# A two-layer diffusion backbone on one core: the modulation loads reordered, and the work at the end of layer 0 and in the second attention placed anew

## The chip, the cores and the metric

The kernel runs on one core of one Trainium2 chip. The metric is the device time of one execution in microseconds (us). A core has a matrix engine (TensorE, PE in the profile), a vector engine (VectorE, DVE), a scalar engine (ScalarE, ACT), a general engine (GpSimd, POOL), and a queue that issues the transfers (SyncE, SP). Each engine runs its own instructions in order; semaphores let one wait for another.

## What is computed

1024 latent tokens and 256 context tokens of width 1024 pass through two layers, in float32. Layer 0 is a global attention A with rotary positions and a banded attention B, side by side; layer 1 is a convolution module C and a neighbourhood attention D with a table of position biases. Only latent tokens leave layer 1, through a last normalisation.

```
for i in range(DEPTH):                       # DEPTH = 2
    sh_l, sc_l, g_l = modulation(c, mod_w[i], mod_b[i])      # silu(cond) @ w + b, in thirds
    sh_c, sc_c, g_c = modulation(c_ctx, mod_w[i], mod_b[i])
    h_lat = rms_norm(x_lat, norm_g[i]) * (1.0 + sc_l) + sh_l
    h_ctx = rms_norm(x_ctx, norm_g[i]) * (1.0 + sc_c) + sh_c
    if i % 2 == 0:
        y_lat, y_ctx = even_mixer(h_lat, h_ctx, ...)   # A and B: projections, softmax(q k) v, gate, @ w_out
    else:
        y_lat, y_ctx = odd_mixer(h_lat, h_ctx, ...)    # C and D: conv + layer norm, attention + bias, gate, @ w_out
    x_lat = x_lat + g_l * y_lat
    x_ctx = x_ctx + g_c * y_ctx              # layer 0 only
return rms_norm(x_lat, final_g)
```

## The kernel before

Every matrix product of the projections is made of three (`mm3`, lines 363 to 365): each factor is split into a rounded high part and the remainder (`split`, lines 334 and 337: hh and hl, wh and wl, ph and pl), and high by high, low by high and high by low are summed. The high part is a copy on ACT; the low part is a subtraction on POOL or DVE.

Tokens go in three chunks, c = 0 (256 context tokens), 1 and 2 (512 latent tokens each). In the opening, x and the modulation weights (mw) arrive by transfers that SP issues, in the order of the letters of `PLAN`: `a`, `b`, `c` and `v` are steps of four slices of the modulation (a capital finishes one), digits load a chunk of x, `n` asks for the squares and sums of a chunk, `w` loads projection weights, `r` makes the broadcast reciprocal root, `H` and `h` make the normalised chunk, `q` projects chunk 0. A chunk's way: squares on ACT (lines 758 to 771), sums acc on DVE or POOL (762, 772), a product with ones on PE (trs), rbv on DVE (293), nr, the power -1/2, on POOL (274), its broadcast bc on PE (299), x·g·bc on DVE (351), and then per block of 128 channels either hh on ACT and hl on DVE (`HV` has a `v`, line 355) or both by `split` on ACT and POOL (`g`). modT is the transposed modulation, made by PE (trm) from mrow, which ACT copies.

Attention (`attn_gen`) runs over groups of tiles. A tile is a score st on PE (lines 531 and 535, from QH, QL and the key table KAt), an exponential pf on ACT, its split ph and pl, and, three tiles later, three products with the values into ov (472 to 474). Every `vshare`-th low part is on DVE, the others on POOL. At the end of a group DVE transposes the sums out of ov (r, line 482), multiplies by the gate (y, or yu in layer 1) and frees the bank. Before a group its maxima are found (`maxes`: products mx on PE, maxima mp on DVE, their negative nmt, transposed by PE, and QL on DVE, line 430; Q goes through memory to QH); this preparation starts `LEAD` tiles after the start of the group two before.

Other work is woven in: `weave(main, n, fill, m)` takes n steps of the attention and spreads m steps of the fill over them: the projections of the next head unit (`NFILL`), the output projection of layer 0 (`O1`), layer 1's projections and output (`WV`, with `LAG`, the number of score tiles that the fill may run ahead). At build time a scheduler fixes each engine's order from these priorities and a simulated clock; `issue_after` forbids an instruction to be placed ahead of another, and `later` lowers the priority. Layer 0 ends with the last attention group, the output projection (po) and, woven into it, the normalised chunks of layer 1; layer 1 has 16 groups.

Of the kernel before, what the change touches and what calls it, by code (L numbers as in the profile page):

```python
# [10 lines left out]
F32 = mybir.dt.float32  # L11
F32R = mybir.dt.float32r
ALU = mybir.AluOpType
# [18 lines left out]
KROWS = ((0, 8), (0, 11), (4, 15), (8, 16))  # L32
BMO = (0, 320, 320, 760)
LOOK0, LOOK1 = 3, 3
LEAD = (3, 4)
AHEAD = 3
BSW, BMW = 768, 1080
CWB = 12
VSH = 5
VORD = (1, 2, 0)  # L40
WBN = 8
VW = 161
TRV = "pp"
HALF = {'half': 3, 'hf': 2}
STG = {"pair": 2, "vT": 1, "spo": 2}
OCE, ODE, OHE = ('v', 'g', 'g')
YB = 1
WPR = 3
VS0 = 12
# [6 lines left out]
PSH = 3  # L56
MODP = ((), (1, 3, 6))
FL = (80, -98)
LAG = (0, 0, 6, 12)
WV = (73, 53, 77, 24, 12)  # L60
SQ = (0, 1)
EV0 = "e0 c0 f0".split()
# [6 lines left out]
def SQT(k, e):  # L69
# [10 lines left out]
GT, G1 = (1, 0)  # L80
EARLY = {2: lambda g, h, c: next(g[0].prep), 4: lambda g, h, c: h(0), 8: lambda g, h, c: c(),
         10: lambda g, h, c: next(g[1].prep), 14: lambda g, h, c: g[0].load_bs(), 18: lambda g, h, c: g[1].load_bs()}
NFILL = (34, 34, 34)
HV = (('gggvvvvg',) * 3, ('gggvvvvg', 'vvvgvvvg', 'gggvvvvg'))
O1 = (6, 134, 14)
TICK0, TICK1 = (1, (8, 6, 16))
PLAN = 'pavaa0vabvnabbvabrbbwcVHcccw1Ch2nrqnh'
LASTN = (2, 2, 3)
MWR = "ABVx"
XA = 4  # L90
ORDER = (2, 3, 0, 1)
QORD = (2, 3, 4, 0, 5, 6, 1, 7, 8, 9)

# [9 lines left out]
def tile_kernel(ctx: ExitStack, tc: tile.TileContext, a, out):  # L103
    nc = tc.nc
    VE, SC, GP, PE, SY = nc.vector, nc.scalar, nc.gpsimd, nc.tensor, nc.sync
# [9 lines left out]
    mk, mwp, hold, layer, spare = [0], [None], [0], [0], []  # L115
# [3 lines left out]
    def bank(tag, name):  # L119
        if tag == "pp" and solo[0] and not sums[0]:  # L120
            turn[0] += 1
            tag = ("pp", "mx")[turn[0] // 2 % 2]
        return ps.tile([P, 512], F32, tag=tag, name=name, bufs=BUFS[tag])
# [3 lines left out]
    def nm(s):  # L127
        uid[0] += 1
        return f"{s}_{uid[0]}"
# [197 lines left out]
    def Hs(h, part, tok, n, dk):  # L327
        c = 0 if tok < 256 else (1 if tok < 768 else 2)
        o = tok - CHUNKS[c][0]
        return h[c][part][:, dk, o : o + n]  # L330

    def split(src, hi, lo, heng="s", leng="g"):
        if heng == "s":
            SC.copy(hi, src)  # L334
        else:
            VE.tensor_copy(hi, src)
        (GP if leng == "g" else VE).tensor_tensor(lo, src, hi.bitcast(F32), op=ALU.subtract)  # L337

    hend = [None, None]

# [5 lines left out]
    def make_h(l, c, xs, bc, h, dks=range(DK)):  # L346

        cond = 1 if c == 0 else 0
        for dk in dks:
            x = xs(dk)  # L350
            VE.scalar_tensor_tensor(x, x, gs[l][:, dk, cond : cond + 1], bc, op0=ALU.mult, op1=ALU.mult)
            shift = modT[l][:, dk, cond : cond + 1]
            if HV[l][c][dk] == "v":
                SC.activation(h[0][:, dk, :], x, AF.Identity, bias=shift)
                hend[0] = VE.scalar_tensor_tensor(h[1][:, dk, :], x, shift, h[0][:, dk, :].bitcast(F32), op0=ALU.add, op1=ALU.subtract)
            else:
                hend[1] = SC.activation(x, x, AF.Identity, bias=shift)
                split(x, h[0][:, dk, :], h[1][:, dk, :])
# [94 lines left out]
    def attn_gen(pool, groups, vshare, look, nexts=None):  # L453

        preps = [g.prep for g in groups]
        items = [(g, t) for g in groups for t in range(len(g.tiles))]
        pend = []
        cnt = [0]

        def flush():  # L460
            g, t, ph, pl = pend.pop(0)
            k, q0, n, _ = g.tiles[t]
            if t == 0:
                g.ov = bank("ov", nm("ov"))
                if g.load_v is not None:
                    g.load_v()
            V, vo = g.v(k)
            vo *= VW
            last = t == len(g.tiles) - 1
            o, ph, pl = cut(g.ov, q0, n), flat(ph, q0, n), flat(pl, q0, n)  # L470
            m = P if t == 0 else VW - 64
            PE.matmul(o[0:m], V[:, vo + 64 : vo + 64 + m], ph, start=(t == 0), stop=False)  # L472
            PE.matmul(cut(g.ov[0:64], q0, n), V[:, vo : vo + 64], ph, start=False, stop=False)  # L473
            pvs.append(PE.matmul(o[0 : VW - 64], V[:, vo + 64 : vo + VW], pl, start=False, stop=(last and g.sink is None)))  # L474
            if last:
                if g.sink is not None:
                    PE.matmul(g.ov, g.skm(), g.QL[0:76, :], start=False, stop=True)
                r1 = pool.tile([P, 8, 32], F32, tag="r1", name=nm("r1"), bufs=1)
                r8 = pool.tile([P, 8], F32, tag="r8", name=nm("r8"), bufs=2)
                rb = pool.tile([P, 256], F32, tag="rb", name=nm("rb"), bufs=1)  # L480
                for e in range(2):
                    VE.transpose(r1[e * 64 : (e + 1) * 64].rearrange("p a b -> p (a b)")
                                 .rearrange("p (a q) -> p a q", a=2), g.den(g.ov[64:128, :], e))
                yu = g.pre(g.ov)
                VE.reciprocal(r8, r1[:, :, 0])
                VE.transpose(rb, r8[:, :, None].broadcast_to([P, 8, 32]))
                g.finish(yu, rb)

        for p in preps[:2]:
            if not layer[0]:  # L490
                next(p)
            yield
        for _ in range(2):
            yield
        for p in preps[:2]:
            for n_, _ in enumerate(p):
                if n_ % 2:
                    yield
        work = []

        def prepare(x, n):

            while n and work and work[0][0] <= x:
                if next(work[0][1], work) is work:
                    work.pop(0)
                else:
                    n -= 1

        for gi, g in enumerate(groups):
            g.ids = [gi + 2] if gi + 2 < len(groups) else []  # L510
            if nexts is not None and gi in nexts:
                g.ids = nexts[gi]
        for g, t in items[:AHEAD]:
            g.ahead(t)
        for x, (g, t) in enumerate(items):
            if x + AHEAD < len(items):
                items[x + AHEAD][0].ahead(items[x + AHEAD][1])
            if t == 0:
                g.start()
                while any(p is g.prep for _, p in work):  # L520
                    prepare(len(items), 1)
                for k in g.ids:
                    next(preps[k])
                    work.append((x + LEAD[layer[0]], preps[k]))
            rate = g.rate * max(len(work), 1)
            k, q0, n, extra = g.tiles[t]
            KA, KB = g.k()
            st = bank("st", nm("st"))
            cs = slice(k * P, (k + 1) * P)
            sf = flat(st, q0, n)  # L530
            sts.append(PE.matmul(sf, KA[:, cs], cut(g.QH, q0, n), start=True, stop=False))  # L531
            if not g.bias:
                for lhs, rhs in extra():
                    PE.matmul(st[:, :n], lhs, rhs, start=False, stop=False)
            PE.matmul(sf, KB[0:68, cs], cut(g.QL[0:68], q0, n), start=False, stop=True)  # L535
            ph = pool.tile([P, 512], F32R, tag="ph", name=nm("ph"), bufs=look + 1)
            pl = pool.tile([P, 512], F32R, tag="pl", name=nm("pl"), bufs=look + 1)
            pf = pool.tile([P, 512], F32, tag="pf" if layer[0] else "ost", name=nm("pf"), bufs=PFB)
            if g.bias and extra is not None:
                VE.tensor_tensor(flat(pf, q0, n), sf, extra(), op=ALU.add)  # L540
                SC.activation(pf[:, :n], pf[:, :n], AF.Exp)
            else:
                SC.activation(pf[:, :n], st[:, :n], AF.Exp, scale=1.0 if g.bias else SCALE)  # L543
            cnt[0] += 1
            split(pf[:, :n], ph[:, :n], pl[:, :n], "s", "v" if cnt[0] % vshare == 0 else "g")
            pend.append((g, t, ph, pl))
            if t == len(g.tiles) // 2:
                g.gate()
            if t == len(g.tiles) - 1:
                g.last()  # L550
            prepare(x, rate // 2)
            yield
            if len(pend) > look:
                flush()
            prepare(x, rate - rate // 2)
            yield
        while pend:
            flush()
            yield
# [32 lines left out]
    h = [None] * 3  # L592
# [130 lines left out]
    with ExitStack() as p0x:  # L723
# [6 lines left out]
        with tc.tile_pool(name="st0", bufs=1, reuse_waits="tile") as st0:  # L730
# [57 lines left out]

            for ev in PLAN:
                if ev in "012":  # L790
# [488 lines left out]
    with ExitStack():  # L1279
# [625 lines left out]
```

## Time and profile before

| | us |
|---|---|
| median of 3 runs (lowest, highest) | 1495.62 (1493.93, 1496.02) |
| the profiled execution | 1491.75 |
| its span in the profile | 1490.0 |
| PE busy in it | 1419.0 |
| DVE, POOL, ACT busy | 1069.9, 821.8, 739.1 |

The profile shows one execution. In a row of the timeline the first number is the start in us from the start of the span, the second the time it took (of all, where a count above one stands at the end as x8), then engine, source line, operation, the tile written and those read, and in brackets the time for which the engine had been idle and what ended that. "trn", "bc", "pl" are names of tiles. A row of waits has the engine, the tile and line that waited, what it waited for, the sum, the count and the longest. A stretch of the table of stages has the busy time and count of each engine, then the clock granted to PE as a share of full speed.

### The profile page before, as it was taken

How to read it: one execution, taken by the hardware profiler on the slowest of the kernel's cores; microseconds unless marked ns; L12 is line 12 of the kernel's file. 1: busy time of each engine (PE TensorE's matmuls, PEld its weight loads, DVE VectorE, ACT ScalarE, POOL GpSimd, SP SyncE). 2: the span in 40 equal slices, each digit the busy share in tenths (PEclk: the TensorE clock that was granted, in tenths of full speed). 3: DMA queues.
4: the chain of work that ended last, by engine and by line, in shares of the span. 5: the costliest groups of instructions: out<-in, count | busy, mean ns of one | idle time of the engine just before them, and what ended most of it. 6: DMA issues, size and time to landing. Idle time of an engine off the chain costs nothing.

```text
span 1490.0 us, 22025 instructions
## 1 busy us (share of the span) xinstructions
PE 1419.0 (95%) x7014; PEld 1146.4 (77%) x7014; DVE 1069.9 (72%) x2126; ACT 739.1 (50%) x1537; POOL 821.8 (55%) x802
## 2 busy tenths in 40 slices
PE   7899999999999999999999989999999999999996
PEld 2898978887888777677887768888777878777775
DVE  4687676588858786667756767999838566668757
ACT  3641453646355765665444645443434354545563
POOL 3561463657456786676554755764544343254673
PEclk9899999999999999999999999999999999999998
DMA  9675145314531235452221221214495867787623
GB/s 351 209 219 164 47 134 177 96 57 151 177 93 36 82 96 161 154 174 85 91 74 45 84 98 58 84 59 121 147 312 178 234 203 223 239 258 226 197 63 120
DMA packets 182922, 215.22 MB, mean 144 GB/s; under 512 B 17292, under 2 KB 136280, under 8 KB 182808
## 3 DMA queue, kind: packets, MB, share of 16 engines
q1 hardware_dynamic: 172560, 195.97, 42.2%
q10 hardware_dynamic: 10248, 17.87, 3.9%
q8 instruction: 55, 0.90, 0.3%
q14 instruction: 59, 0.48, 0.1%
HBM read 151.64 MB, written 62.13 MB: 143 GB/s over the span
## 4 chain that ended last, share of the span: by engine, by line
PE 74%; DVE 8%; DMA 7%; issue 4%; POOL 4%; ACT 2%; SPq 0%; DVEq 0%; POOLq 0%; ACTq 0%
PE p L363 7%; PE p L365 7%; PE p L364 7%; PE ov L472 4%; PE ov L474 4%; PE st L531 4%; PE ov L473 4%; PE st L535 4%; PE po L363 4%; PE po L365 3%; PE po L364 3%; PE pq L365 3%; PE pq L363 3%; PE pq L364 3%; PE pg L363 2%
## 5 line engine op out<-in xcount | busy, mean ns | idle before, releaser
L337 POOL TENSOR_TENSOR pl<-pf,ph 128x512 fp32r<-128x512 f32 (+3 forms) x321 | 391.6, 1235 | 263.8 <-ACT ph L334 213.4
L337 POOL TENSOR_TENSOR wl<-wr,wh 128x256 fp32r<-128x256 f32 (+2 forms) x253 | 193.9, 786 | 136.9 <-ACT wh L334 105.7
L543 ACT ACTIVATE pf<-st 128x512 f32<-128x512 f32 x284 | 165.6, 597 | 158.9 <-PE st L535 141.6
L334 ACT CAST ph<-pf 128x512 fp32r<-128x512 f32 (+3 forms) x364 | 204.3, 579 | 18.2 <-PE ov L473 8.6
L363 PE MATMUL p<-hh,wh 128*128 128x512 f32 x448 | 176.7, 396 | 3.5 <-ACT vT L1405 1.4
L364 PE MATMUL p<-hl,wh 128*128 128x512 f32 x448 | 177.2, 397 | 0.0
L365 PE MATMUL p<-hh,wl 128*128 128x512 f32 x448 | 174.2, 398 | 0.1
L334 ACT CAST wh<-wr 128x256 fp32r<-128x256 f32 (+2 forms) x260 | 100.8, 404 | 135.0 <-DMA wr<-in_od_d_dram 31.9
L472 PE MATMUL ov<-ph,Vt 128*97 128x512 f32 (+4 forms) x364 | 138.4, 381 | 12.7 <-DVE y L700 4.2
L474 PE MATMUL ov<-pl,Vt 128*97 128x512 f32 (+3 forms) x364 | 138.4, 381 | 5.2 <-POOL pl L337 2.6
L531 PE MATMUL st<-QH,KAt 128*128 128x512 f32 (+3 forms) x364 | 139.7, 385 | 2.5 <-ACT pf L543 0.9
L473 PE MATMUL ov<-ph,Vt 128*64 128x512 f32 (+3 forms) x364 | 135.9, 373 | 0.0
L535 PE MATMUL st<-QL,KBt 68*128 68x512 f32 (+3 forms) x364 | 134.6, 378 | 1.2 <-DVE QL L430 1.2
L658 DVE TENSOR_REDUCE mp<-mx 128x1 f32<-128x512 f32 x128 | 86.0, 683 | 57.6 <-PE mx L657 57.0
L1296 DVE SCALAR_TENSOR_TENSOR cps<-U,taps,cps 128x512 f32<-128x512 f32 x184 | 124.4, 747 | 0.0
L363 PEld LDWEIGHTS p<-hh,wh 128*128 128x128 f32 x448 | 84.2, 188 | 23.1 <-ACT wh L334 2.0
L365 PEld LDWEIGHTS p<-hh,wl 128*128 128x128 f32 x448 | 84.2, 188 | 20.7 <-POOL wl L337 1.0
L364 PEld LDWEIGHTS p<-hl,wh 128*128 128x128 f32 x448 | 84.2, 188 | 20.0 <-issue 0.5
L363 PE MATMUL pq<-wh,hh 128*128 128x384 f32 x256 | 88.6, 346 | 1.1 <-ACT pc L923 1.1
L365 PE MATMUL pq<-wh,hl 128*128 128x384 f32 x256 | 87.8, 344 | 1.8 <-POOL hl L337 1.8
L364 PE MATMUL pq<-wl,hh 128*128 128x384 f32 x256 | 88.3, 345 | 0.0
L472 PEld LDWEIGHTS ov<-ph,Vt 128*97 128x97 f32 (+1 forms) x364 | 60.9, 167 | 32.4 <-issue 8.2
(300 smaller groups left out, 3413.4 us busy)
## 6 DMA issues: line engine op xcount, KB each, us to landing
mw<-in_mod_w_dram SPq DMA_DIRECT2D x28, 512.0 KB, 5.9
Q<-qs SPq DMA_DIRECT2D x40, 256.0 KB, 2.7
QH<-Q SPq DMA_DIRECT2D x80, 128.0 KB, 2.8
bm<-in_d_bm_dram SPq DMA_DIRECT2D x16, 540.0 KB, 5.6
wr<-in_od_d_dram SPq DMA_DIRECT2D x64, 128.0 KB, 2.6
wr<-in_ev_qkv_dram SPq DMA_DIRECT2D x32, 192.0 KB, 4.5
QD<-spq SPq DMA_DIRECT2D x48, 128.0 KB, 2.5
KAt<-KD SPq DMA_DIRECT2D x8, 768.0 KB, 7.5
```

Of the source, the lines that this page charges most:

```text
L334: SC.copy(hi, src)
L337: (GP if leng == "g" else VE).tensor_tensor(lo, src, hi.bitcast(F32), op=ALU.subtract)
L363: PE.matmul(o, lh, rh, start=first, stop=False)
L364: PE.matmul(o, lh, rl, start=False, stop=False)
L365: done[0] = PE.matmul(o, ll, rh, start=False, stop=last)
L472: PE.matmul(o[0:m], V[:, vo + 64 : vo + 64 + m], ph, start=(t == 0), stop=False)
L473: PE.matmul(cut(g.ov[0:64], q0, n), V[:, vo : vo + 64], ph, start=False, stop=False)
L474: pvs.append(PE.matmul(o[0 : VW - 64], V[:, vo + 64 : vo + VW], pl, start=False, stop=(last and g.sink is None)))
L531: sts.append(PE.matmul(sf, KA[:, cs], cut(g.QH, q0, n), start=True, stop=False))
L535: PE.matmul(sf, KB[0:68, cs], cut(g.QL[0:68], q0, n), start=False, stop=True)
L543: SC.activation(pf[:, :n], st[:, :n], AF.Exp, scale=1.0 if g.bias else SCALE)
L1296: VE.scalar_tensor_tensor(pc, uc, w, pc, op0=ALU.mult, op1=ALU.add)
```

## The change

It changes numbers that steer the order, and a few lines.

```
-LEAD = (3, 4)                      +LEAD = (3, 7)
-VSH = 5                            +VSH = 7
-OCE, ODE, OHE = ('v', 'g', 'g')    +OCE, ODE, OHE = ('g', 'g', 'g')
-LAG = (0, 0, 6, 12)                +LAG = (0, 0, 3, 18)
-NFILL = (34, 34, 34)               +NFILL = (34, 34, 37)
-HV = (... ('gggvvvvg', 'vvvgvvvg', 'gggvvvvg'))
+HV = (... ('gggvvvvg', 'vvvvgvvg', 'gggvvgvg'))
-O1 = (6, 134, 14)                  +O1 = (6, 137, 14)
-PLAN = 'pavaa0vabvnabbvabrbbwcVHcccw1Ch2nrqnh'
+PLAN = 'pavva0avnbababrvbbabVcHwccwc1nCh2rqhn'
-XA = 4                             +XA = 2
```

`PLAN`: the v slice alternates with a and b, and the squares (`n`) are asked for earlier. `XA`: a load of x or weights is placed behind the last two, not four, modulation products. `LEAD`: in layer 1 the maxima start seven tiles in. `VSH`: every seventh low part of layer 1 is on DVE, not every fifth (16 of 112 rather than 22). `OCE`: the eight subtractions that split the conv output (oc, 128x512 each) go from DVE to POOL. (`AHEAD`, 3 to 4, steers a step that does nothing.) The code:

```
     def split(src, hi, lo, heng="s", leng="g"):
...
-            SC.copy(hi, src)
+            cast[0] = SC.copy(hi, src)
...
+        i_ = (GP if leng == "g" else VE).tensor_tensor(lo, src, hi.bitcast(F32), op=ALU.subtract)
+        cast[2 if leng == "g" else 1] = i_
...
+            bound = tailc if l == 1 and c == 1 and dk >= 5 else [None] * 3
+            with ExitStack() as cx:
+                for b_ in bound:
+                    if b_ is not None:
+                        cx.enter_context(tc.issue_after(b_.ins))
+                make_h1(l, c, dk, x, shift, h)
...
-                g.ov = bank("ov", nm("ov"))
+                g.ov = bank("mx" if g is groups[-1] and not layer[0] else "ov", nm("ov"))
...
+            tailc[:] = cast
```

So the last blocks of the normalised chunk 1 of layer 1 stand behind the last attention tile's split on each engine, and the last group of layer 0 has an ov bank of its own.

Three places show what moves. First the opening on DVE: acc_422 and acc_385 are the sums of chunk 1, before and now, acc_523 and acc_551 those of chunk 2, xr_382 is chunk 1 of x. Before:

```order
L772 TENSOR_TENSOR acc_422<-acc_422,sq_442 128x512
L293 TENSOR_SCALAR rbv_450<-trs_445 128x4
L762 TENSOR_TENSOR acc_523<-acc_523,sq_525 128x512
L762 TENSOR_TENSOR acc_523<-acc_523,sq_528 128x512
L762 TENSOR_TENSOR acc_523<-acc_523,sq_531 128x512
L351 SCALAR_TENSOR_TENSOR xr_382<-xr_382,gs_92,bc_454 128x512 x8
```

And now, on the same engine:

```order
L785 TENSOR_TENSOR acc_385<-acc_385,sq_405 128x512
L293 TENSOR_SCALAR rbv_450<-trs_445 128x4
L856 CAST bmt<-cst 128x256
L857 CAST sk<-cst 76x128
L775 TENSOR_TENSOR acc_551<-acc_551,sq_553 128x512
L355 SCALAR_TENSOR_TENSOR xr_382<-xr_382,gs_92,bc_454 128x512 x8
L775 TENSOR_TENSOR acc_551<-acc_551,sq_556 128x512
L367 SCALAR_TENSOR_TENSOR hl_170<-xr_382,modT_90,hh_169 128x512 x2
L775 TENSOR_TENSOR acc_551<-acc_551,sq_559 128x512
```

Two of the three sums of chunk 2 went behind the products; two small casts came ahead of them. On POOL, nr_452 had two sums of chunk 2 ahead of it and has one.

Second, the end of layer 0 on DVE: hl_9722 is the low part of layer 1's chunk 1, pl_9625 that of the last attention tile. Before:

```order
L293 TENSOR_SCALAR rbv_9543<-trs_9538 128x4
L351 SCALAR_TENSOR_TENSOR x_1825_7287<-x_1825_7287,gs_93,bc_9716 128x512 x8
L355 SCALAR_TENSOR_TENSOR hl_9722<-x_1825_7287,modT_91,hh_9721 128x512 x3
L337 TENSOR_TENSOR pl_9625<-pf_9626,ph_9624 128x512
L355 SCALAR_TENSOR_TENSOR hl_9722<-x_1825_7287,modT_91,hh_9721 128x512 x3
L482 STREAM_TRANSPOSE r_2468_9642<-ov_9525 64x256 x2
```

And now, on the same engine:

```order
L293 TENSOR_SCALAR rbv_9546<-trs_9541 128x4
L340 TENSOR_TENSOR hl_7310<-y_9485,hh_7309 128x2x128
L355 SCALAR_TENSOR_TENSOR x_1825_7287<-x_1825_7287,gs_93,bc_9716 128x512 x8
L367 SCALAR_TENSOR_TENSOR hl_9722<-x_1825_7287,modT_91,hh_9721 128x512 x4
L340 TENSOR_TENSOR pl_9625<-pf_9626,ph_9624 128x512
L367 SCALAR_TENSOR_TENSOR hl_9722<-x_1825_7287,modT_91,hh_9721 128x512 x2
L494 STREAM_TRANSPOSE r_2468_9642<-ov_9513 64x256 x2
```

Four hl stand ahead of the last low part and two behind it. On PE bc_9716 stood 15 rows ahead of the product with pl_9625 and now stands 25 ahead. POOL's part there, before:

```order
L337 TENSOR_TENSOR pl_9472<-pf_9473,ph_9471 128x512
L337 TENSOR_TENSOR pl_9508<-pf_9509,ph_9507 128x512
L337 TENSOR_TENSOR pl_9533<-pf_9534,ph_9532 128x512
L274 TENSOR_TENSOR nr_9545<-rbv_9543,mhalf 128x4
L1219 TENSOR_TENSOR acc_2448_9561<-acc_2448_9561,sq_2455_9591 128x256
L337 TENSOR_TENSOR pl_9554<-pf_9555,ph_9553 128x512
```

And now, on POOL:

```order
L340 TENSOR_TENSOR pl_9472<-pf_9473,ph_9471 128x512
L274 TENSOR_TENSOR nr_9548<-rbv_9546,mhalf 128x4
L340 TENSOR_TENSOR pl_9508<-pf_9509,ph_9507 128x512
L1232 TENSOR_TENSOR acc_2448_9564<-acc_2448_9564,sq_2455_9591 128x256
L340 TENSOR_TENSOR pl_9533<-pf_9534,ph_9532 128x512
L340 TENSOR_TENSOR pl_9554<-pf_9555,ph_9553 128x512
```

nr went ahead of two low parts. Third, near the end of layer 1's attention on DVE: r_3934 and yu_15758 free the ov bank, QL_15489 is the last group's table. Before:

```order
L419 TENSOR_REDUCE nmt_15692<-mp_15599 128x4
L540 TENSOR_TENSOR pf_15745<-st_15740,bs_15484 128x256
L430 TENSOR_TENSOR QL_15489<-trn_15710,k_bd 4x512
L337 TENSOR_TENSOR pl_15731<-pf_15732,ph_15730 128x128
L482 STREAM_TRANSPOSE r_3934_15753<-ov_15585 64x256 x2
L1546 SCALAR_TENSOR_TENSOR yu_15758<-ov_15585,gt_3885_15577 64x256 x2
```

And now, on the same engine (yu_15756, QL_15474):

```order
L552 TENSOR_TENSOR pf_15741<-st_15736,bs_15438 128x256
L494 STREAM_TRANSPOSE r_3933_15751<-ov_15586 64x256 x2
L1559 SCALAR_TENSOR_TENSOR yu_15756<-ov_15586,gt_3885_15578 64x256 x2
L431 TENSOR_REDUCE nmt_15746<-mp_15688 128x4
L552 TENSOR_TENSOR pf_15771<-st_15766,bs_15438 128x384
L497 RECIPROCAL r_3934_15752<-r_3933_15751 128x8
```

r and yu come ahead of nmt, and QL_15474 follows some rows later.

More of the change, by code (lines that the diff above doesn't have):

```diff
@@ L34 @@
 LOOK0, LOOK1 = 3, 3
-LEAD = (3, 4)
-AHEAD = 3
+LEAD = (3, 7)
+AHEAD = 4
 BSW, BMW = 768, 1080
 CWB = 12
-VSH = 5
+VSH = 7
 VORD = (1, 2, 0)
@@ L45 @@
 STG = {"pair": 2, "vT": 1, "spo": 2}
-OCE, ODE, OHE = ('v', 'g', 'g')
+OCE, ODE, OHE = ('g', 'g', 'g')
 YB = 1
@@ L58 @@
 FL = (80, -98)
-LAG = (0, 0, 6, 12)
+LAG = (0, 0, 3, 18)
 WV = (73, 53, 77, 24, 12)
@@ L82 @@
          10: lambda g, h, c: next(g[1].prep), 14: lambda g, h, c: g[0].load_bs(), 18: lambda g, h, c: g[1].load_bs()}
-NFILL = (34, 34, 34)
-HV = (('gggvvvvg',) * 3, ('gggvvvvg', 'vvvgvvvg', 'gggvvvvg'))
-O1 = (6, 134, 14)
+NFILL = (34, 34, 37)
+HV = (('gggvvvvg',) * 3, ('gggvvvvg', 'vvvvgvvg', 'gggvvgvg'))
+O1 = (6, 137, 14)
 TICK0, TICK1 = (1, (8, 6, 16))
-PLAN = 'pavaa0vabvnabbvabrbbwcVHcccw1Ch2nrqnh'
+PLAN = 'pavva0avnbababrvbbabVcHwccwc1nCh2rqhn'
 LASTN = (2, 2, 3)
 MWR = "ABVx"
-XA = 4
+XA = 2
 ORDER = (2, 3, 0, 1)
@@ L330, in Hs @@
         return h[c][part][:, dk, o : o + n]
+    cast = [None] * 3
+    tailc = [None] * 3
     def split(src, hi, lo, heng="s", leng="g"):
         if heng == "s":
-            SC.copy(hi, src)
+            cast[0] = SC.copy(hi, src)
         else:
             VE.tensor_copy(hi, src)
-        (GP if leng == "g" else VE).tensor_tensor(lo, src, hi.bitcast(F32), op=ALU.subtract)
+        i_ = (GP if leng == "g" else VE).tensor_tensor(lo, src, hi.bitcast(F32), op=ALU.subtract)
+        cast[2 if leng == "g" else 1] = i_
     hend = [None, None]
@@ L352, in make_h, with make_h1 @@
             shift = modT[l][:, dk, cond : cond + 1]
+            bound = tailc if l == 1 and c == 1 and dk >= 5 else [None] * 3
[4 more added lines that the diff above has]
+                make_h1(l, c, dk, x, shift, h)
+    def make_h1(l, c, dk, x, shift, h):
             if HV[l][c][dk] == "v":
```

## The prediction, made before the changed kernel was run

> **What bounds the kernel now.** I read the page first (shares and chain), then a table of stages, then the waits of TensorE (PE) and the timeline where its idle time sits. The share of each engine and the chain that ended last:
>
> ```profile
> PE 1419.0 (95%) x7014; PEld 1146.4 (77%) x7014; DVE 1069.9 (72%) x2126; ACT 739.1 (50%) x1537; POOL 821.8 (55%) x802
> PE 74%; DVE 8%; DMA 7%; issue 4%; POOL 4%; ACT 2%; SPq 0%; DVEq 0%; POOLq 0%; ACTq 0%
> ```
>
> PE is busy for all but 71 us of 1490. The change removes no matmul, so it can win only there, and in the stretches in which the clock is low. The table of stages says where (the columns after the stretch are busy us of PE, PEld, DVE, ACT, POOL, then clock, DMA share, GB/s):
>
> ```profile
> 0.00:50.00 50.00, 38.81 (x141) 16.49 (x141) 27.03 (x60) 24.38 (x53) 16.92 (x24) 1.00 1.01 358
> 75.00:125.00 50.00, 47.62 (x284) 43.83 (x284) 45.52 (x85) 16.45 (x39) 26.57 (x39) 1.00 0.75 224
> 470.00:840.00 370.00, 359.21 (x1703) 276.85 (x1702) 258.14 (x441) 209.11 (x392) 242.55 (x194) 1.00 0.33 103
> 840.00:905.00 65.00, 57.64 (x278) 45.98 (x277) 40.98 (x68) 35.17 (x74) 38.34 (x41) 0.95 0.24 79
> 1155.00:1455.00 300.00, 286.37 (x1464) 231.28 (x1463) 203.86 (x496) 158.31 (x359) 147.24 (x174) 0.99 0.67 204
> 1455.00:1490.00 35.00, 23.17 (x148) 19.98 (x147) 25.00 (x63) 9.79 (x25) 12.94 (x15) 0.88 0.36 128
> ```
>
> Idle PE in these rows: 11.2 us up to 50, then 2.4, 10.8, 7.4, 13.6 and 11.8 us; the stretches left out hold the rest. The conv stretch, 905 to 1155, is reordered only slightly: nothing, by PE's work on both sides of it.
>
> **The opening.** Up to 50 us the transfers are the limit (share 1.01), and the bytes ahead of x stay the same; so x lands when it did, near 35.9, where ScalarE (ACT) takes the first square. What then counts is the way from the squares to the product x·g·rstd (line 351) that lets the projections of chunk 1 begin:
>
> ```profile
> 35.93 0.63 ACT L768 ACTIVATE acc<-xr 128x512 f32<-128x512 f32 x1 [2.20 <-DMA xr<-in_xT_dram]
> 38.03 0.56 ACT L202 COPY mrow<-pm 2x512 f32<-2x512 f32 x1
> 41.45 0.17 DVE L210 TENSOR_TENSOR modT<-trm,modb 128x8 f32<-128x8 f32 x1 [1.02 <-PE trm L206]
> 44.73 0.68 DVE L772 TENSOR_TENSOR acc<-acc,sq 128x512 f32<-128x512 f32 x1
> 47.03 0.16 DVE L293 TENSOR_SCALAR rbv<-trs 128x4 f32<-128x4 f32 x1 [1.62 <-PE trs L288]
> 47.21 1.29 POOL L762 TENSOR_TENSOR acc<-acc,sq 128x512 f32<-128x512 f32 x1
> 48.45 1.48 POOL L274 TENSOR_TENSOR nr<-rbv,mhalf 128x4 f32<-128x4 f32 x1
> 49.98 1.16 PE L299 MATMUL bc<-ident,nr 128*128 128x128 f32 x8 [1.83 <-POOL nr L274]
> 49.74 2.37 DVE L762 TENSOR_TENSOR acc<-acc,sq 128x512 f32<-128x512 f32 x2 [0.69 <-ACT sq L761]
> 52.03 5.35 DVE L351 SCALAR_TENSOR_TENSOR xr<-xr,gs,bc 128x512 f32<-128x512 f32 x8
> ```
>
> Three delays stand in it. (1) The seven sums end at 45.41. Eight squares of 0.63 from 35.93 and one addition of 0.68 could end at 41.65; the copy at 38.03 and the wait for modT stand among them. With the modulation copy ahead of the squares I take half of the 3.8 us, 1.9. (2) nr could start when rbv is there, 47.19; it starts at 48.45, behind a chunk-2 sum: 1.26. In the new order one chunk-2 sum is still ahead of it, which should be done by then. (3) The products could start when bc ends, 51.14; the sums of chunk 2 hold them to 52.03: 0.89. One such sum (0.68) remains ahead in the new order, the others come behind. Sum 1.9 + 1.26 + 0.89 - 0.68 = 3.4. Bounds: 0, if SP's later issue of x (two more modulation tiles stand ahead in its queue) leaves the transfers idle for that time, and 3.8 + 1.26 + 0.89 = 5.9. From 55 us on PE runs these projections without long stops, and their order up to 500 us hardly changes, so the lead should last. I take **3.4**.
>
> **Third head unit.** The projections of the fourth unit are woven into the third in 37 rather than 34 parts of the same stretch, so they end some 9 us sooner, by its main steps of about 1 us. There PE waits for the key table:
>
> ```profile
> 608.32 0.77 PE L657 MATMUL mx<-KAt,QH 128*128 128x512 f32 x1 [1.40 <-DMA KAt<-K]
> 608.88 0.63 PE L474 MATMUL ov<-pl,Vt 128*97 128x512 f32 x1
> 609.31 0.63 PE L472 MATMUL ov<-ph,Vt 128*97 128x512 f32 x1
> ...
> 850.12 0.40 PE L472 MATMUL ov<-ph,Vt 128*97 128x512 f32 x1
> 850.35 0.40 PE L473 MATMUL ov<-ph,Vt 128*64 128x512 f32 x1
> ...
> L337 POOL TENSOR_TENSOR pl<-pf,ph 128x512 fp32r<-128x512 f32 (+3 forms) x321 | 391.6, 1235 | 263.8 <-ACT ph L334 213.4
> ```
>
> The wait (1.40) goes; the matmuls behind it start 0.43 us apart (608.88, 609.31) where 0.23 is usual (850.12, 850.35), for about seven of them: 1.5 us. Against that, low parts (pl) stand denser on POOL, whose splits average 1.235 us: one late piece costs 1.2. Ends -1.2 and +2.9; I take **1.5**, nearer the wait itself.
>
> **End of layer 0.** The normalised chunk 1 for layer 1 is made while the last attention tiles run:
>
> ```profile
> 850.01 1.02 POOL L274 TENSOR_TENSOR nr<-rbv,mhalf 128x4 f32<-128x4 f32 x1
> 851.75 1.05 PE L299 MATMUL bc<-ident,nr 128*128 128x128 f32 x8
> 852.84 5.36 DVE L351 SCALAR_TENSOR_TENSOR x<-x,gs,bc 128x512 f32<-128x512 f32 x8 [4.32 <-PE bc L299]
> 858.11 2.07 DVE L355 SCALAR_TENSOR_TENSOR hl<-x,modT,hh 128x512 fp32r<-128x512 f32 x3
> 860.10 0.68 DVE L337 TENSOR_TENSOR pl<-pf,ph 128x512 fp32r<-128x512 f32 x1
> 860.84 0.74 PE L474 MATMUL ov<-pl,Vt 128*97 128x512 f32 x1 [2.38 <-DVE pl L337]
> 860.70 4.11 DVE L355 SCALAR_TENSOR_TENSOR hl<-x,modT,hh 128x512 fp32r<-128x512 f32 x3
> 859.52 4.08 POOL L337 TENSOR_TENSOR hl<-x,hh 128x512 fp32r<-128x512 f32 x2 [2.81 <-ACT hh L334]
> 864.82 0.92 DVE L482 STREAM_TRANSPOSE r<-ov 64x256 f32<-64x256 f32 x2
> 867.19 0.38 PE L363 MATMUL po<-hc,wh 128*128 128x256 f32 x1 [1.60 <-DVE x L1185]
> 870.76 1.54 PE L363 MATMUL po<-hh,wh 128*128 128x512 f32 x3 [1.91 <-ACT hh L334]
> ```
>
> The last tile's low part pl is queued on VectorE (DVE) behind eleven long instructions that wait for bc; the reader is to see PE stop for it, and again twice for what follows it (transposes r, then y, then hh). In the new order bc stands ten attention matmuls of 0.233 us nearer the front, 2.3 us; four hl rather than three stand ahead of pl (+0.69), two rather than three behind it (4.11 / 3 = 1.37 less). So pl is 2.3 - 0.7 = 1.6 us sooner, r 1.6 + 1.4 = 3.0, and the last wait with it, less what POOL's turns take from it. nr has two POOL low parts fewer ahead of it, and these come behind it, where the tiles need them: one of 1.2 late. Ends: -1.2, and 2.38 + 1.60 + 1.91 = 5.9, all three waits. I take **2.5**.
>
> **Layer-1 attention.** Its maxima start seven rather than four tiles into the group before; six low parts and the eight splits of the conv output move from DVE to POOL. PE's waits there, and the longest case:
>
> ```profile
> PE ov L472 <- DVE yu L1546: 3.4, 2, 2.5
> ...
> PE mx L1520 <- DMA QH<-QD: 1.5, 1, 1.5
> ...
> 1419.76 0.68 DVE L430 TENSOR_TENSOR QL<-trn,k_bd 4x512 fp32r<-4x512 f32 x1
> 1422.85 0.47 PE L472 MATMUL ov<-ph,Vt 128*128 128x512 f32 x1 [2.45 <-DVE yu L1546]
> ```
>
> Before the 2.45 us wait nmt, QL and a low part stand ahead of r and yu on DVE; the new order has r and yu first, which I price at half of the 3.4 us: 1.7. Fourteen subtractions cost DVE 14 x 0.68 = 9.5 us less and POOL 14 x 1.235 = 17.3 us more, beside 300 - 147 = 153 us in which POOL is idle; 0.5 for what of it comes late. Ends: -14 x (1.235 - 0.68) = -7.8, and 3.4 + 1.5 = +4.9. I take **1.2**.
>
> **Tail.** rbv of the last half comes behind two x and two wl on DVE, but nine matmuls and three x are moved ahead of bc; 35 us with 12 idle hide neither surely. **0**, ends -2 and +2.
>
> [...] After the 1.40 us wait above the matmuls ran at half pace, and the stretch behind the 2.38 us wait was granted
>
> ```profile
> 860.00:864.00 4.00, 3.17 (x14) 3.07 (x15) 4.00 (x4) 1.30 (x3) 3.60 (x2) 0.58 0.08 20
> ```
>
> a clock of 0.58. [...]
>
> **Sum.** 3.4 + 1.5 + 2.5 + 1.2 + 0 = 8.6. The profiled execution took 1491.75 us (span 1490.0 and 1.75 around it), so 1483.1 for such a run; it lies 3.87 below the median of the runs shown, 1495.62, so against that **1487.0**. Own range: the three longest ways to an upper end halved, 3.7 + 3.4 + 2.5, give 4.8; the two longest to a lower end halved, 9.0 + 3.7, give 6.3: 1482 to 1493.
>
> **Rivals.**
> A, layer 1 gives the gain back through turns of DVE and POOL. Between 859.52 and 864.82 the two hl of POOL and DVE's three and the pl took 5.30 us; one by one they take 2 x 1.235 + 2.07 + 0.68 = 5.22. So the two engines excluded each other there. Each subtraction moved to POOL would then hold DVE for 1.235 instead of 0.68: 7.8 us, if all land where DVE is late. 1487.0 + 1.2 + 7.8 = 1496.0, no change. For it: those rows; against it: DVE is idle 96 of 300 us, and its maxima read PSUM. [...]
> B, the slower side: the maxima of layer 1 come too late. Three tiles later means the table QH (stored, loaded again) arrives later at each of 14 groups. The one wait of this kind now costs 1.5. At 14 x 0.9 = 12.6 us it decides: 1487.0 + 1.2 + 12.6 = 1500.8; from 10.5 us on the kernel is slower by over 0.2%. For it: with r and yu moved ahead near 1420, nmt and QL of the last group come behind them. Against it: in the new order most maxima stand, counted in rows, about where they stood.
> C, the opening does not move: the transfers, or x, set the time, as the wait of 2.20 at 35.93 would have it. 1487.0 + 3.4 = 1490.4.
> D, the gains come whole and the clock stays up: the upper ends lie 2.5, 1.4, 3.4 and 3.7 above the terms taken, 11.0 together; half of that gives 1481.5.
>
> **Chances.** Forecast 0.50, A 0.16, B 0.10, C 0.14, D 0.10. About 0.2%, 3.0 us, is what a measurement tells from no change: below 1492.6 faster, above 1498.6 slower. C and D are faster, A the same but for its edges: faster 0.74, same 0.16, slower 0.10. Range 1479 to 1498: D's lower half lies at its low end, and only B and the worst of the bounds are left out above.
>
> **What would show it.** In the new profile: L351 of chunk 1 at 48 to 49 rather than 52.03, with nr 1.3 us or less behind rbv; no wait for KAt near 600; the last low part of layer 0 leaving PE idle under 1 us, and the two waits behind it about 3 us sooner; the wait for yu near 1420 under 1 us. PE idle in the layer-1 stretch above 16 us, with POOL or QH as releaser, would prove me wrong by A or B; L351 still at 52, by C.

## The result and the profile after

The mean of six runs of the changed kernel is 1480.7 us, that of seven runs of the kernel before, beside them, 1492.8 us: a ratio of 0.9919, 95% interval 0.9893 to 0.9946, or 12.1 us less. A seventh run of the changed kernel took 1616.71 us at a granted clock of 0.81, a slow state of the chip, and is left out of the ratio; with it the median is 1481.70 us. 1487.0 was forecast, 8.6 less than the median of 1495.62 shown ahead of the prediction. The profiled execution of the changed kernel took 1486.05 us (span 1484.1), the slowest of the six; the next section says by what the runs of one kernel differ. Its busy time, and the same stages as shown of before (columns as there):

```profile
PE 1420.0 (96%) x7014; PEld 1152.5 (78%) x7014; DVE 1066.0 (72%) x2111; ACT 745.4 (50%) x1538; POOL 827.8 (56%) x817
```

```profile
0.00:50.00 50.00, 40.09 (x147) 18.25 (x148) 28.03 (x61) 23.50 (x52) 17.15 (x23) 0.98 1.00 351
75.00:125.00 50.00, 47.50 (x273) 43.10 (x273) 45.25 (x83) 13.45 (x34) 24.35 (x46) 0.97 0.77 225
470.00:840.00 370.00, 359.50 (x1708) 277.88 (x1707) 262.19 (x443) 211.93 (x393) 243.28 (x194) 1.00 0.33 103
840.00:905.00 65.00, 60.01 (x292) 48.30 (x291) 45.12 (x79) 40.27 (x86) 42.20 (x43) 0.95 0.25 79
1155.00:1455.00 300.00, 286.47 (x1467) 235.18 (x1465) 201.67 (x488) 162.66 (x361) 156.75 (x188) 0.98 0.65 200
```

Of the stages shown the one with clearly less idle PE is the end of layer 0, 5.0 us against 7.4; layer 1's attention looks as idle as before, 13.5 us against 13.6. That would credit the one with all it seems to have won and the other with nothing, from one execution of each kernel. In the kernel with the opening alone changed (below), whose order at the end of layer 0 is that of before, the same 65 us read

```profile
836.00:901.00 65.00, 59.84 (x288) 47.73 (x287) 43.05 (x78) 38.63 (x81) 39.78 (x42) 0.95 0.25 79
```

5.2 us idle: a difference of 2.4 us can stand between two executions of the same order, and so is no proof of the change.

The opening, chunk 1 of x:

```profile
40.43 0.91 ACT L366 ACTIVATE hc<-xr,modT 128x256 fp32r<-128x256 f32 x2 [1.89 <-DVE modT L210]
46.88 0.16 DVE L293 TENSOR_SCALAR rbv<-trs 128x4 f32<-128x4 f32 x1 [1.42 <-PE trs L288]
47.27 1.06 POOL L274 TENSOR_TENSOR nr<-rbv,mhalf 128x4 f32<-128x4 f32 x1
48.39 2.08 PE L299 MATMUL bc<-ident,nr 128*128 128x128 f32 x8 [1.09 <-POOL nr L274]
50.51 5.36 DVE L355 SCALAR_TENSOR_TENSOR xr<-xr,gs,bc 128x512 f32<-128x512 f32 x8 [1.61 <-DMA gr<-in_ev_g_dram]
```

nr follows rbv at once, as forecast, but rbv is only 0.15 us sooner, and bc takes 2.08 us instead of 1.16: PE's clock was halved from 48.4 on (0.50 granted between 48.39 and 50.51). The products start at 50.51 rather than 52.03. The row names the transfer of gr as what DVE waited for; bc ended at 50.47, and the products need it, so I take bc to be what held them.

The end of layer 0, first DVE, POOL and PE of the changed kernel:

```profile
849.04 5.05 POOL L340 TENSOR_TENSOR pl<-pf,ph 128x512 fp32r<-128x512 f32 x4
849.24 5.36 DVE L355 SCALAR_TENSOR_TENSOR x<-x,gs,bc 128x512 f32<-128x512 f32 x8 [2.36 <-PE bc L299]
857.16 0.69 DVE L340 TENSOR_TENSOR pl<-pf,ph 128x512 fp32r<-128x512 f32 x1
855.79 3.18 POOL L340 TENSOR_TENSOR pl<-pf,ph 128x512 fp32r<-128x512 f32 x1 [1.70 <-ACT ph L337]
859.03 0.74 PE L486 MATMUL ov<-pl,Vt 128*97 128x512 f32 x1 [2.56 <-POOL pl L340]
867.56 0.96 PE L375 MATMUL po<-hh,wh 128*128 128x512 f32 x3 [0.82 <-ACT hh L337]
```

DVE's last low part is earlier, but PE stops as long as before (2.56 against 2.38 us): the last low part on POOL (four before it took 5.05 / 4 = 1.26 us each) took 3.18 beside DVE's hl, and is now what PE waits for. The two waits behind it went from 1.60 + 1.91 to 0.82. Over all profiles of this study the same holds: with the old order of this place (nine profiles) the stop is 1.91 to 2.40 us and the waits behind it add to 1.2 to 3.6, with the new order, whole or in part (five), the stop is 1.64 to 3.06 and the waits behind it 0 to 0.8.

### The profile page after: what moved, and what is told of

It reads as the page before. It is cut to its first block, busy times and chain, and to the rows that moved or that the text cites. A ratio compares the mean times of both kernels' runs of the same rounds, so it can differ in the third digit from the quotient of the medians.

```text
span 1484.1 us, 22019 instructions
## 1 busy us (share of the span) xinstructions
PE 1420.0 (96%) x7014; PEld 1152.5 (78%) x7014; DVE 1066.0 (72%) x2111; ACT 745.4 (50%) x1538; POOL 827.8 (56%) x817
## 4 chain that ended last, share of the span: by engine, by line
PE 72%; DMA 13%; DVE 7%; ACT 3%; issue 2%; POOL 2%; SPq 1%; ACTq 0%; DVEq 0%; POOLq 0%
PE p L375 6%; PE p L376 6%; PE p L377 5%; PE ov L484 4%; PE ov L486 4%; PE st L543 4%; PE ov L485 4%; PE st L547 4%; PE po L375 4%; PE po L376 4%; PE po L377 4%; PE pq L375 3%; PE pq L376 3%; PE pq L377 3%; PE pg L375 2%
## 5 line engine op out<-in xcount | busy, mean ns | idle before, releaser
L340 POOL TENSOR_TENSOR pl<-pf,ph 128x512 fp32r<-128x512 f32 (+1 forms) x327 | 392.4, 1213 | 243.4 <-ACT ph L337 201.9
L377 PEld LDWEIGHTS p<-hh,wl 128*128 128x128 f32 x448 | 84.2, 188 | 19.9 <-issue 0.7
L543 PEld LDWEIGHTS st<-QH,KAt 128*128 128x128 f32 x364 | 69.1, 190 | 25.3 <-ACT pf L555 10.5
```

What stands on the lines that cost most here:

```text
L340: i_ = (GP if leng == "g" else VE).tensor_tensor(lo, src, hi.bitcast(F32), op=ALU.subtract)
L377: done[0] = PE.matmul(o, ll, rh, start=False, stop=last)
```

## The clock, read over many runs

The trace records when the clock granted to PE was halved (from about 10 us after the start on). In all fourteen profiles of this study these stretches are 3.41 us long or a whole number of such (the last is cut by the end), and within one run they lie on one grid of 3.41 us; from run to run the grid sits elsewhere against the start (a cell begins at 850.59 us in the changed kernel, at 849.30 with O1 put back). Cut along it, the end of layer 0 in the changed kernel reads (busy PE is the second number):

```profile
850.59:854.01 3.42, 3.10 (x13) 1.45 (x11) 3.42 (x7) 3.42 (x7) 3.42 (x3) 1.00 0.00 0
854.01:857.42 3.41, 1.17 (x3) 0.38 (x3) 3.41 (x6) 3.41 (x8) 1.71 (x2) 0.99 0.07 19
857.42:860.83 3.41, 1.80 (x4) 1.24 (x5) 3.41 (x3) 1.69 (x4) 3.41 (x3) 0.50 0.00 0
860.83:864.25 3.42, 3.42 (x18) 3.40 (x17) 3.19 (x8) 0.42 (x1) 1.52 (x1) 0.51 0.13 38
864.25:867.66 3.41, 2.59 (x23) 2.38 (x21) 2.99 (x8) 1.13 (x3) 0.84 (x3) 1.00 0.02 5
```

A cell with 1.17 us of work is followed by one at half clock, that one has 1.80 and is followed by another at half clock, that one has 3.42 and the clock is back. Counted over all cells that ran at full clock, but for the first and the last of each record: of 39 with PE busy for under 45% every one was followed by half clock, of 140 between 45% and 65% 47 were, of 217 between 65% and 80% 8, and of 5467 above that none. So two microseconds of idle PE in one cell leave it 41% busy, among the 39 that were all followed by half clock: if PE has work for all of the next cell, that costs half of 3.41, 1.7 us (an estimate), and more if a second cell follows. Spread evenly over two cells the same idle leaves each 71% busy, and only 8 of 217 such cells were followed by half clock.

Every run has a mean clock and a span, so its time can be split: (1 - clock) x span is what the clock took if PE were the only limit, and the rest is work and waits. The clock is recorded to a thousandth, so one run's split is good to 0.7 us; and the two parts are not independent, since of the cells at full clock only those in which PE idled were followed by half clock (none of the 5467 above 80% busy).

| kernel | runs | mean us | taken by the clock | rest |
|---|---|---|---|---|
| before | 30 | 1493.9 | 20.6 | 1473.3 |
| changed | 6 | 1480.7 | 21.5 | 1459.3 |
| opening alone | 12 | 1490.6 | 19.9 | 1470.8 |
| third unit alone | 12 | 1491.7 | 21.0 | 1470.7 |
| end of layer 0 alone | 12 | 1496.4 | 25.8 | 1470.7 |
| layer 1 alone | 7 | 1485.4 | 15.5 | 1469.9 |
| LEAD 7 alone | 12 | 1493.3 | 19.1 | 1474.2 |
| moved subtractions alone | 12 | 1490.5 | 20.6 | 1469.9 |
| LAG alone | 12 | 1494.3 | 23.0 | 1471.3 |
| changed, end of layer 0 put back | 6 | 1476.8 | 14.8 | 1462.1 |
| changed, only HV put back | 4 | 1477.4 | 19.2 | 1458.2 |
| changed, only O1 put back | 4 | 1473.1 | 14.0 | 1459.1 |
| changed, only bank and last blocks put back | 4 | 1477.2 | 15.5 | 1461.7 |

The row of the kernel before is of the 30 runs beside the first four parts. In the 29 beside LEAD, the moves and "end of layer 0 put back" it had 20.8 and 1473.6, in the 17 beside LAG and the single pieces put back 19.7 and 1472.9. The standard error of a difference between two rows is about 1 us in either column, up to 1.8 where there are few runs.

Over the changed kernel's runs the rest has a standard deviation of 1.2 us, the time one of 3.5: they differ mostly by the clock. (Before: 2.5 and 3.7; layer 1 alone: 3.8 and 3.5, so there not.)

## The experiments

Each ratio is to the kernel before, run beside it on the same chip. The first four are the kernel before with one part of the change.

**Opening alone.**

```
-PLAN = 'pavaa0vabvnabbvabrbbwcVHcccw1Ch2nrqnh'      -XA = 4
+PLAN = 'pavva0avnbababrvbbabVcHwccwc1nCh2rqhn'      +XA = 2
```

> The kernel before with only the order of the opening changed (PLAN and XA). Theory: the opening's lead, 3.2 us with the half-rate stretches of the clock counted out (about 1.9 to 3.0 as it stands at 130 us), is made by 55 us, carries to the end, and is independent of the rest: ratio about 0.998, L351 of chunk 1 at 50 to 51 us rather than 52.03. Rival: it is given back where the matrix engine waits for something that comes at its own time (tables, weights), and the end does not move: ratio 1.000, the lead seen at 100 us gone by 500.

0.9974 (0.9951 to 0.9996), 3.9 us. The products start at 49.58, 2.5 us sooner than before, bc taking its usual time:

```profile
48.38 1.16 PE L299 MATMUL bc<-ident,nr 128*128 128x128 f32 x8 [1.10 <-POOL nr L274]
49.58 5.36 DVE L351 SCALAR_TENSOR_TENSOR xr<-xr,gs,bc 128x512 f32<-128x512 f32 x8 [0.70 <-PE bc L299]
```

Matched matmul by matmul against the profile before, its lead is 4.2 us at 70, 4.1 at 500 and 3.9 at 800 us: the opening's lead carries through 700 us of almost unchanged order. What is more than 2.5 came between 60 and 66 us. There PE waited before for a low part of POOL

```profile
61.54 0.44 PE L365 MATMUL pq<-wh,hl 128*128 128x384 f32 x1 [1.78 <-POOL hl L337]
```

(0.90 to 2.03 us in all eight profiles with the old opening, no such wait in the six with the new one), and ran at half clock from 62.0 to 65.4, as three of the other seven with the old opening did there and four did not: up to 1.7 us of this lead may be the luck of that pair. Behind 800 us the scheduler places layer 1 differently: the lead rises to 9.5 us by 1200, and 6 us are lost by 1245, up to 3.4 of them in a half-clock stretch from 1200 to 1207. At the end this profile is 1.5 us longer than that of before (span 1491.5 against 1490.0); the 3.9 us are of the averages. So the theory holds up to layer 1; "independent of the rest" does not.

**End of layer 0 alone.**

```
-HV[1][1], HV[1][2] = 'vvvgvvvg', 'gggvvvvg'       -O1 = (6, 134, 14)
+HV[1][1], HV[1][2] = 'vvvvgvvg', 'gggvvgvg'       +O1 = (6, 137, 14)
+ the casts kept in `tailc`, the last blocks of chunk 1 issued behind them
+ g.ov = bank("mx" if g is groups[-1] and not layer[0] else "ov", nm("ov"))
```

> The kernel before with only the end of layer 0 changed (HV, the order of the last blocks behind the last tile, the ov bank of the last group, O1). Theory: the lead grows by 3 to 4 us between 845 and 900 us with the clock counted out, and some of the 2.4 us that the changed kernel won in the conv stretch comes with it: ratio 0.996 to 0.998. Rival: the lead there comes from work that the third unit's denser fill brought forward, and alone this part brings under 1 us: ratio 0.999 to 1.000.

1.0016 (0.9997 to 1.0034): no gain, and a loss is not clear of zero. Alone it does not move nr ahead of the low parts, and one more hl (0.69 us) stands ahead of the last low part, so PE stops 3.06 us instead of 2.38:

```profile
859.72 0.69 DVE L340 TENSOR_TENSOR pl<-pf,ph 128x512 fp32r<-128x512 f32 x1
860.46 0.74 PE L486 MATMUL ov<-pl,Vt 128*97 128x512 f32 x1 [3.06 <-DVE pl L340]
```

The next wait is 0.68 us, where before two of 1.60 and 1.91 stood. By the table this part saves 2.6 us of waits and the clock takes 5.2 more. Neither theory had that.

**Layer 1 alone.**

```
-LEAD = (3, 4)   -VSH = 5   -OCE = 'v'   -LAG = (0, 0, 6, 12)
+LEAD = (3, 7)   +VSH = 7   +OCE = 'g'   +LAG = (0, 0, 3, 18)
```

> The kernel before with only layer 1's attention changed (LEAD, VSH, OCE, LAG). Theory: 3 to 4 us with the clock counted out, between 1155 and 1450 us: ratio 0.997 to 0.998. Rival (the prediction's A and B): moved subtractions and later maxima cost as much as they bring, and what the changed kernel won there came from the conv stretch: ratio 1.000 or above.

0.9939 (0.9916 to 0.9962), 9.1 us: the largest part. The theory's 3 to 4 us were meant with the clock counted out, and by the table work and waits are 3.4 us shorter, as it said; the other 5.1 are the clock's, and no theory had them. The rival (moved subtractions and later maxima cost what they bring) is out. The four parts add to -0.26 + 0.16 - 0.61 - 0.15 = -0.86%, and together they gave -0.81%.

**Third unit alone.**

```
-NFILL = (34, 34, 34)
+NFILL = (34, 34, 37)
```

> The kernel before with only the third unit's fill denser (NFILL 37). Theory: 1.3 us with the clock counted out, no wait for KAt near 608: ratio 0.999. Rival: the denser low parts on GpSimd give it back at 500 to 530 us and at 635, and the end does not move: ratio 1.000.

0.9985 (0.9968 to 1.0002), 2.2 us, not clear of zero. The wait for KAt is gone, here and in the changed kernel. Another has come 26 us later, 2.03 us here; in the changed kernel it reads

```profile
634.41 0.50 PE L543 MATMUL st<-QH,KAt 128*128 128x512 f32 x1 [2.58 <-ACT pf L555]
```

The next three take layer 1 apart.

**LEAD 7 alone, and LEAD 10** (`LEAD = (3, 7)`, `(3, 10)` in the kernel before).

> The kernel before with only LEAD changed for layer 1, 4 to 7 tiles. Theory: the table's transfer is asked for at the start of a group, and the maxima that read it come LEAD tiles later; four tiles are about as long as the transfer takes beside the bias and key tables, seven are longer. So the waits of the maxima on QH (1.5, 4.5, 6.3 and 3.6 us in the four profiles with LEAD 4) fall under 2 us, and most of the 9.1 us of the layer-1 part comes with it: ratio 0.994 to 0.997. Rival: the subtractions moved from VectorE to GpSimd free VectorE, and LEAD alone brings nothing: ratio 0.999 to 1.002.

> The kernel before with LEAD 10 in layer 1. Theory (room for the transfer): the waits on QH stay under 2 us as with 7, the time is that of LEAD 7 within 3 us, unless nmt and QL, made later still, come too late for the group (waits of st on QL). Rival (luck of the order): waits on QH come back at other groups, the ratio is 0.998 to 1.002. Rival (the prediction's B, maxima too late): slower, above 1.003, with PE waiting for nmt, trn or QL in most groups.

0.9991 (0.9977 to 1.0005) and 1.0002 (0.9985 to 1.0018). PE's waits in layer 1, first of the opening alone (LEAD 4), then of LEAD 7:

```profile
PE mx L1520 <- DMA QH<-QD: 4.5, 4, 1.8
PE ov L472 <- DVE yu L1546: 2.8, 2, 2.4
```

```profile
PE ov L472 <- DVE yu L1546: 5.1, 2, 3.7
PE p L363 <- ACT wh L334: 2.1, 2, 1.3
```

With LEAD 7 0.2 us of waiting on QH is left, with LEAD 10 0.7. The waits went as the theory has it, and the time did not: PE stops for DVE instead, 3.7 us in one place. Nor did a trace show the lengths that the theory names: in the profile before, the table's transfer (QH<-QD) took 3.3 to 7.7 us to land, and 110 score tiles start between 1155 and 1455 us, 2.7 us each, so about 10.9 us for four (an estimate). Nor is it shown that LEAD is what governs the waits: with LEAD 4 they are 0.6 us with the moves alone and none is listed with LAG alone, and with LEAD 7 they are 1.8 with all of layer 1 changed. The maxima are not too late either, so the prediction's B is out even at 10.

**The moved subtractions alone** (`VSH = 7`, `OCE = 'g'` in the kernel before).

> The kernel before with only the fourteen subtractions of layer 1 moved from VectorE to GpSimd (VSH, OCE). Theory: VectorE was not what the maxima waited for, and the two engines take turns: no change, ratio 0.998 to 1.002, waits on QH still 1.5 to 6 us. Rival: the gain of the layer-1 part is in them, 0.994 to 0.997. The prediction's A would have them cost up to 7.8 us: 1.005.

0.9972 (0.9954 to 0.9989), 4.2 us: the theory was wrong, and A with its loss of 7.8 us too. Waiting for yu, 3.4 us before, 2.8 and 5.1 in the two profiles above, falls to 0.7, and that for QH to 0.6:

```profile
PE ov L472 <- DVE yu L1546: 0.7, 1, 0.7
PE mx L1520 <- DMA QH<-QD: 0.6, 1, 0.6
```

By the table all of the gain is in work and waits (3.7 us beside its own kernel before). So VectorE was what the attention waited for, and freeing it counts, though its busy time fell by only 4.4 us (1069.9 to 1065.5 in the two profiles) where 14 subtractions of 0.68 are 9.5.

**LAG alone** (`LAG = (0, 0, 3, 18)`).

> The kernel before with only LAG changed. The layer-1 part gave 0.9939, the moved subtractions 0.9972 and LEAD 0.9991, together 0.9963. Theory (sums): LAG brings the rest, ratio 0.997 to 0.999. Rival (interplay): LAG alone brings nothing, 0.999 to 1.002, and the rest comes only where the three stand together.

1.0010 (0.9997 to 1.0023): nothing. LEAD, moves and LAG add to -0.27%, together they gave -0.61%. The difference is 0.34%, and the half widths of the four intervals, added in squares, come to 0.35%: interplay is possible and not shown. The split says where it would lie. Against the kernel before run beside each, work and waits change by +0.6 (LEAD), -3.7 (moves) and -1.6 us (LAG), -4.7 in sum, and by -3.4 with all three together: no surplus. The clock takes -1.7, -0.2 and +3.3, +1.4 in sum, and -5.1 together. So what the whole of layer 1 brings beyond its pieces is in the clock, not in waits that one piece uncovers and another takes away. With all three the waits read

```profile
PE mx L1520 <- DMA QH<-QD: 1.8, 1, 1.8
PE ov L472 <- DVE nmt L419: 1.4, 1, 1.4
```

The last four put the end of layer 0 back in the changed kernel, whole and by pieces.

**All of it put back.**

> The changed kernel with only the end of layer 0 put back (HV, O1, the ov bank, the blocks behind the last tile). Theory: that part brings nothing that can be measured, since the stop ahead of the last tile's product stays (2.56 us, now for GpSimd's low part): the ratio is that of the changed kernel, 0.990 to 0.993, or a little better, as the part alone gave 1.0016. Rival (the prediction's term): it brings 2.5 us in the presence of the others: 0.9935 to 0.9945.

0.9882 (0.9854 to 0.9910), 1476.72 us: about what theory said at best. It reads lower than the changed kernel, but the two intervals overlap. Work and waits are 2.8 us longer, the clock takes 6.7 us less.

**HV put back** (`'vvvgvvvg', 'gggvvvvg'` in the changed kernel).

> The changed kernel with HV put back: which blocks of layer 1's chunks 1 and 2 GpSimd splits. The end-of-layer-0 part saved 2.7 us of waits and cost 5 to 7 us of clock in the two pairs of kernels measured. Theory: the clock was lost at the chunks that HV touches (half-rate stretches at 857 to 864 and near 1127): mean clock 0.988 or more, time 3 us or more under the changed kernel's 1481, ratio 0.989 or under. Rival: it is O1 that does it, and here the clock stays at 0.985 to 0.986, ratio 0.991 to 0.993.

0.9898 (0.9880 to 0.9915), clock 0.987: both lie between the two forecasts, and the interval overlaps that of the changed kernel, so it is not to be told from it.

**O1 put back** (`O1 = (6, 134, 14)` in the changed kernel).

> The changed kernel with O1 put back to 134. On GpSimd nr comes one low part later again, so bc does. Theory (clock lost through HV or the new bank): the stop before the last tile's product grows by up to 1.2 us, time as the changed kernel or 1 to 2 us longer, clock 0.985 to 0.986: ratio 0.992 to 0.994. Rival (O1 costs the clock): mean clock 0.988 or more and ratio 0.989 or under.

0.9869 (0.9853 to 0.9885), 1473.33 us, clock 0.9905: the rival's numbers came, and this is the fastest kernel of the study, some 7.5 us under the changed one by the two ratios. Its interval lies wholly under the changed kernel's. nr does come a low part later, and yet PE stops for less:

```profile
845.26 6.27 POOL L340 TENSOR_TENSOR pl<-pf,ph 128x512 fp32r<-128x512 f32 x5
854.54 0.68 DVE L340 TENSOR_TENSOR pl<-pf,ph 128x512 fp32r<-128x512 f32 x1
855.27 0.48 PE L486 MATMUL ov<-pl,Vt 128*97 128x512 f32 x1 [1.64 <-DVE pl L340]
```

POOL's last low parts run here while DVE waits for bc or makes its products, 1.25 us each, and are done at 851.5; with O1 137 the last of them stands beside DVE's hl and takes 3.18. After 130 us this run was at half clock only three times, at 631, 856 and in the tail from 1464, against eight times in the changed kernel's profile. Work and waits in sum are alike (1459.1 against 1459.3).

**Bank and last blocks put back** (the shared ov bank, no rule on the last blocks).

> The changed kernel with the shared ov bank and without the rule that the last blocks come behind the last tile: now six hl, not four, stand ahead of the last low part on VectorE. Theory: the stop there grows by 2 x 0.69 to 1.4 us or more (to about 3.5 to 4 us), in one piece, which drops the clock to half for at least one stretch of 3.41 us wherever it falls: 1 to 4 us slower than the changed kernel, 0.992 to 0.995. Rival: the bank costs more than the rule brings, and it is 1 us or more faster.

0.9893 (0.9874 to 0.9912): the expected loss did not come. The stop was 2.51 us, with 1.67 ahead of it, half clock for 10.2 us there. That a stop of 3.5 to 4 us halves the clock wherever it falls was my estimate, and this run did not test it; one of 3.66 us, with LEAD 7 alone, ended at 1211.86 and was followed by matmuls of 512 columns 0.43 us apart, where 0.23 is usual. In the averages the rest is 2.4 us longer and the clock takes 6.0 less than in the changed kernel. That fits the clock being lost over the whole of the kernel that follows, by how idle time falls, and not at this one stop. Putting back HV, O1 and the bank one at a time takes 2.3, 7.5 and 6.0 us off the clock's part, 15.8 in sum, and putting back all three takes off 6.7. So it is not shown that O1 by itself costs clock: over the orders in the table the clock took between 14.0 and 25.8 us, and 21.5 with the changed kernel's, more than with any of the four that put a part of it back (14.0 to 19.2).

## Why the prediction was right in sum, and where not

The time, its sign and its size were right: 8.6 us forecast, 12.1 measured. The terms were not all.

- **Opening**, 3.4: right in size (alone 3.9 by time, 2.5 of it work and waits; up to 1.7 of the 4.1 us of lead at 500 is clock, as said above). The step inside was off: of its three delays (3) went, (2) went for the most part (nr 0.23 us behind rbv where it had been 1.26), and (1) brought 0.15 where 1.9 was taken: ACT had a copy fewer among the squares but waited 1.89 us for modT before the next. The products came 1.5 us sooner, 2.5 where the clock did not slow bc, not 3.4; the rest came behind them, in PE's wait for POOL's hl at 61.54, which the prediction had not named, and in the clock. In the changed kernel's own profile the lead is 3.0 us at 100 and gone by 400: it was at half clock at 120 and at 342, for 3.41 us each, where the profile before was not.
- **Third head unit**, 1.5: 2.2 measured, with an interval that takes in 1.5 and zero. The KAt wait went as said; a wait of 2.58 us for pf came, a place the prediction had not named, which may be the denser fill's cost. (The term's seven slowed matmuls at 0.20 us come to 1.4, not 1.5.)
- **End of layer 0**, 2.5: wrong at the stop, right in the sum of waits, wrong in the time. The arithmetic for DVE held (pl was due 1.6 us sooner against its surroundings and came about 1.5 sooner: 2.9 less the lead of 1.4 that the two products ahead of it had), but the term assumed that PE would wait for DVE still. POOL's low part took its place, 3.18 us long. That is rival A's mechanism, turns of DVE and POOL, at a place where I had priced it as "1.2 late". In waits the part did save the 2.5 (2.6 and 2.8 in the two pairs), but behind the stop, not in it; what it cost in clock, 5 to 7 us, had no term.
- **Layer 1**, 1.2: mis-sized, 9.1 measured, 3.4 of it work and waits. The failing step is the one which took 0.5 us of cost for the moved subtractions and half of the waits for yu, 1.7, as gain: alone they gave 4.2. I counted the waits of one execution and took them for the kernel's. That profile showed 1.5 us of waits on QH; three other kernels with LEAD 4 showed 3.6 to 6.3, and two 0.6 or none. The larger miss is the clock, which takes 5 us less with the new layer 1 alone and had no term.
- **Tail**, 0: the two waits there are 1.27 and 2.84 us in both profiles. Right.
- **A** was wrong for layer 1 and right for the end of layer 0; layer 1's maxima, which it named against itself, were not held up (in the profile before, mp at L1522 took a median of 0.69 us both in the 12 cases with no such work on POOL beside it and in the 11 with POOL subtracting or adding for over nine tenths of it; that PSUM is the reason was not shown). **B** was wrong at LEAD 7 and 10, **C** wrong: the first square began no sooner (36.35 against 35.93) and the lead came all the same. **D** had the clock stay up; it did not in the changed kernel, but with O1 put back the ratio reads 19.6 us, near the 11.0 + 8.6 of all upper ends.

Of the signs that the prediction set out, nr behind rbv, the wait for KAt and the wait for yu (0.9 us in sum, 0.5 at most) came; L351 of chunk 1 came at 50.51, not at 48 to 49, and the last low part left PE idle for 2.56 us, not for under 1.

The total came out near partly by luck. In work and waits the four parts take off 2.5 (opening), 2.6 (third unit), 2.6 (end of layer 0) and 3.4 us (layer 1), 11.1 in sum, and the whole change about 14: the prediction's four terms are of that size, layer 1's the furthest off. The clock, for which it had no term, takes 5.2 more with the end of layer 0 alone and 5.1 less with layer 1 alone, and about 1 more with the whole change: these stand against each other.

What stays open: why a piece of the end of layer 0, O1 above all, changes how often the clock falls in layer 1, 300 us later. Each kernel has one profile, and the order there differs in many rows at once.

## What to carry to other kernels

When a scheduler fixes the order, an edit is not local: in its profile the opening's 4 us held as long as the order behind it was the same, and where it was not, the lead rose to 9.5 us and then fell to nothing. So price an edit by its own stretch, but judge it by runs, and put each part back in the full change as well as testing it alone; here that found a kernel 7.5 us faster. Split the time of every run into the clock's part and the rest before crediting an edit: the waits said what each part did, and the clock added or took as much again. And a wait that is gone from the list need not be time won: with LEAD alone the waits on QH fell to 0.2 us, PE stopped for DVE instead, and the time stayed.

## What the runs showed of the hardware

In these fourteen profiles the clock granted to PE changes on a grid of cells of 3.41 us, and it went with how busy PE was within a cell: all 39 at full clock and under 45% busy were followed by half clock, of the 5467 above 80% none. By the split it took 14 to 26 us of these kernels, and two kernels with equal work and waits (1459.1 and 1459.3 us) differ by 7.5 us through it alone. At the end of layer 0 in the changed kernel DVE and POOL took turns: a subtraction of 1.26 us on POOL took 3.18 us beside DVE's hl. Beside DVE's products x·g·bc, whose bc PE had made, they did not in the same profile: four low parts took 1.26 us each on POOL while the eight products took 0.67 each (5.36 / 8).
